# Ninety-six unused bytes: the output stages' left-hand tiles move from 384 to 480 modulo 512

## The chip, the cores and the metric

The kernel runs on one core of one Trainium2 chip. A core has a matrix engine (TensorE, in the profile PE, with its weight loads shown apart as PEld), VectorE (DVE), ScalarE (ACT), GpSimd (POOL) and SyncE (SP), which here issues most of the transfers. [...] The metric is the device time of one execution in microseconds (us).

## The reference, cut to what matters

One layer of a decoder block on 2048 tokens of width 1024. The input is normalised and projected by one wide matrix (`z`); its columns feed a convolution branch and an attention branch. What matters here is the end, where the two branches are projected, gated, added and projected again:

```python
h = rms_norm(x, norm_w) * (1 + scale) + shift
z = h @ w_in                                  # a, b, g_conv, q, k, v, g_attn, m_conv, m_attn
u = silu(layer_norm(causal_conv(a * sigmoid(b)))) * silu(g_conv)
o = attention(q, k, v) * silu(g_attn)         # three dilated windows, merged by their softmax sums
y_conv = u @ w_conv_out                       # 2048 x 1024 by 1024 x 1024
y_attn = o @ w_attn_out                       # 2048 x 512 by 512 x 1024
y = sigmoid(m_conv) * y_conv + sigmoid(m_attn) * y_attn
x = x + gate * (y @ w_out)                    # 2048 x 1024 by 1024 x 1024
```

All inputs and outputs are float32.

## The kernel before, in words

**Precision.** Every large product is made of three passes in a rounded float32 type: each operand is split into a high and a low part (ScalarE copies the high part, VectorE or GpSimd subtracts), and high x high, high x low and low x high are added up in one PSUM bank. So 512 columns of a result over a depth of 128 cost three matmuls of a 128x128 stationary tile against a 128x512 moving tile.

**Stages.** First the projection for q, k, v with attention beside it (matmuls of line 371, moving tiles 384 wide). Then the projections for the gates and for the convolution's input, in blocks by a Strassen-like scheme with seven products (line 897). Then the output stages, with which this case is concerned:

- *Attention projection*, `ya`, line 1203 through the helper `project`: four token blocks `t` of 512 by eight row blocks `dm`; each is 4 x 3 = 12 matmuls, with weights `wah`/`wal` stationary and `ai` moving. The `ai` of block 0 lies in `ai0`, a reused quarter of the hT pools; those of blocks 1 to 3 come from the pools `ua` and `ub` by `parts`.
- *Convolution projection*, `yc`, the same helper: four token blocks by eight row blocks, 8 x 3 = 24 matmuls each, with `wc0` and `wc1` stationary and `u` moving. `u` comes out of the class `Norm` (load, mean, variance, spread, apply), whose steps are hung between the matmuls of the blocks before by `at_block`. `spread` has small matmuls of its own, `pr` (line 1248), that wait for a power computed by GpSimd (`stf`, line 115) from a VectorE copy (line 1241).
- *Output projection*, `oa`, `ob`, `oc`, line 1485: eight quads of seven products with 12 matmuls each; the split `y` is stationary, the weights `wo` are moving. Of the seven weights, B21 and T1 lie in the pool `op`; the others in quarters of the hT pools, in `wcp` and in `lnp`.

**Order.** TensorE's order is the written one (`manual_schedule`). The other engines' queues are ordered by a planner with a simulated timeline, which sees each tile's dependencies; a new tile waits for the old tiles that lay on its bytes (`reuse_waits="tile"`). SyncE issues loads and stores in one queue, so a store that waits for its data holds up the loads behind it.

**Layout.** Pools are stacked from both ends of SBUF. Most open on the left and grow upwards; those with `side="right"` grow downwards from the top. In the layout of the kernel before, the left stack starts at byte 128 with the constants, which have several small tiles and end at 6,016; `sum` takes 8,192 more, up to 14,208, which is 384 modulo 512. When the convolution's pools (`cv`, `gpa`) close at line 1171, the output stages' left-hand pools open from 14,208 on: `gt`, `fr`, `ys`, `ub`, `ua`, and last `ap` (up to 129,120) or, later, `op` in the place of `ua` and `ap`. All tiles below `ap` are multiples of 2,048 bytes, so every matmul operand in `ub`, `ua` and `op` starts at 384 modulo 512. The right stack starts at 229,344, which is 480 modulo 512, and holds tiles of multiples of 512 bytes: all operands of lines 371 and 897, and in the output stages `ai0`, `wah`, `wal`, `wc0`, `wc1` and five of the seven `wo`. Its lowest pool in the output stages is `lnp`, from 131,040.

The matmul of the helper `project`:

```python
        terms = [t for k in range(len(wh)) for t in ((wh[k], xh[k]), (wh[k], xl[k]), (wl[k], xh[k]))]
        for m, (w, xx) in enumerate(terms):
            nc.tensor.matmul(pz, w, xx, start=(m == 0), stop=(m == len(terms) - 1))
```

## Time and profile before

| what | value |
|---|---|
| median of 3 runs | 2399.38 us (2398.85 to 2400.38) |
| profiled execution: time, span | 2401.62 us, 2399.8 us |
| granted TensorE clock, mean | 0.993 |
| TensorE busy | 2356.1 us, 98% |
| VectorE, ScalarE, GpSimd busy | 72%, 43%, 35% |
| first `ya` / first `yc` / first `oa` | 1952 / 2052 / 2240 us |

The profiled execution's span runs from its first to its last instruction. TensorE's matmuls are pipelined: one begins before the one ahead of it has ended, so the duration of a matmul is longer than the spacing from one to the next. The spacing can be read from the chain of work that ended last, where a piece stands for a row of matmuls one behind the other: its length divided by their number. In the groups of instructions, a name such as `ya<-ai_0h,wah` is the result, the moving tile and the stationary tile, with buffer numbers left out.

### The profile page before, as it was taken

To read this page: it belongs to the slowest core of one execution; us is meant where nothing else is said; L and a number is where in the kernel's file an instruction comes from. 1 tells how busy PE (TensorE), PEld (TensorE's weight loads), DVE (VectorE), ACT (ScalarE), POOL (GpSimd) and SP (SyncE) were. 2 spreads that over 40 slices of the span, in tenths; PEclk is the share of its full clock that TensorE was granted. 3 is DMA by queue.
4 is the path that set the end of the run, shared out by engine and by line. 5 is a ranking of instruction groups with operands and counts; after the bars stand their busy time and mean duration, and the time that the engine had idled before them with its cause. 6 is when DMAs were issued, how large, how long until landed. Compare 5 with 4: busy or idle time off the path is not lost.

```text
span 2399.8 us, 38725 instructions
## 1 busy us (share of the span) xinstructions
PE 2356.1 (98%) x12353; PEld 2089.2 (87%) x12353; DVE 1738.8 (72%) x4091; ACT 1022.4 (43%) x2850; POOL 842.7 (35%) x1003
## 2 busy tenths in 40 slices
PE   6999999999999999999999999999999999999999
PEld 2989999999999999998888888788888888878887
DVE  5865655655556777777699999979968778787544
ACT  4733433333444454456444444644444444332221
POOL 3421111111111111123667779656556730000221
PEclk8999999999999999999999999999999999999999
DMA  7633544555552222134545455745444579866552
GB/s 258 216 118 105 163 124 143 155 151 155 165 161 79 65 79 62 55 108 156 169 133 176 154 158 193 239 127 152 141 149 132 167 228 319 288 230 200 177 158 101
DMA packets 354105, 378.56 MB, mean 158 GB/s; under 512 B 29736, under 2 KB 251208, under 8 KB 353902
## 3 DMA queue, kind: packets, MB, share of 16 engines
q1 hardware_dynamic: 316414, 316.64, 42.4%
q10 hardware_dynamic: 37488, 59.46, 7.3%
q8 instruction: 98, 1.61, 0.3%
q14 instruction: 105, 0.86, 0.1%
HBM read 235.34 MB, written 140.64 MB: 157 GB/s over the span
## 4 chain that ended last, share of the span: by engine, by line
PE 87%; DVE 3%; DMA 2%; ACT 2%; issue 1%; POOL 1%; SPq 0%; ACTq 0%; DVEq 0%; POOLq 0%
PE pz L371 29%; PE paab L897 7%; PE yc L1203 6%; PE oa L1485 4%; PE ya L1203 4%; PE pcab L897 4%; PE pag_mc_d L897 4%; PE pag_g_d L897 3%; PE pag_ma_d L897 3%; PE po L500 3%; PE ps L451 3%; PE oc L1485 2%; PE pcg_g_d L897 2%; PE pcg_mc_d L897 2%; PE paag L897 2%; PE pbab L897 2%
## 5 line engine op out<-in xcount | busy, mean ns | idle before, releaser
L371 PE MATMUL pz<-wh_u,hT_lo 128*128 128x384 f32 x1536 | 536.8, 350 | 5.4 <-DVE hT_lo L290 3.6
L371 PE MATMUL pz<-wh_u,hT_hi 128*128 128x384 f32 x1536 | 518.7, 338 | 4.8 <-ACT wh_u L347 2.4
L371 PE MATMUL pz<-wl_u,hT_hi 128*128 128x384 f32 x1536 | 519.2, 338 | 0.4 <-DVE wl_u L350 0.4
L114 POOL TENSOR_SCALAR st<-st 128x2 f32<-128x2 f32 x192 | 48.6, 253 | 809.8 <-ACT sq L388 809.8
L402 DVE SCALAR_TENSOR_TENSOR qk<-pz,st,wqk 128x128 f32<-128x128 f32 x384 | 116.9, 346 | 270.7 <-POOL st L115 269.6
L371 PEld LDWEIGHTS pz<-wh_u,hT_hi 128*128 128x128 f32 x1536 | 291.0, 189 | 8.0 <-ACT wh_u L347 3.3
L371 PEld LDWEIGHTS pz<-wh_u,hT_lo 128*128 128x128 f32 x1536 | 290.0, 189 | 8.3 <-DVE hT_lo L290 4.6
L371 PEld LDWEIGHTS pz<-wl_u,hT_hi 128*128 128x128 f32 x1536 | 290.0, 189 | 1.6 <-DVE wl_u L350 1.1
L443 ACT ACTIVATE qkT<-ptq 128x256 f32<-128x256 f32 x192 | 73.5, 383 | 358.3 <-PE ptq L436 304.0
L975 DVE SCALAR_TENSOR_TENSOR ce<-us,pair_taps,ce 128x512 f32<-128x512 f32 x240 | 180.6, 753 | 6.5
L946 DVE SCALAR_TENSOR_TENSOR ce<-ut,chan,ce 128x512 f32<-128x512 f32 x240 | 178.7, 745 | 0.0
L861 POOL TENSOR_TENSOR slT<-wT,shT 128x512 fp32r<-128x512 f32 x107 | 143.7, 1344 | 81.0 <-ACT shT L860 81.0
L959 DVE SCALAR_TENSOR_TENSOR cq<-ut,chan,cq 128x512 f32<-128x512 f32 x208 | 155.2, 746 | 1.0
L860 ACT ACTIVATE shB<-wB 128x512 fp32r<-128x512 f32 x130 | 82.0, 631 | 162.7 <-PE paab L897 51.7
L115 POOL TENSOR_TENSOR st<-st,mhalf 128x2 f32<-128x2 f32 x192 | 137.3, 715 | 16.0
L388 ACT ACTIVATE sq<-pz 128x128 bf16<-128x128 f32 x384 | 105.6, 275 | 87.5 <-PE pz L371 78.5
L860 ACT ACTIVATE shT<-wT 128x512 fp32r<-128x512 f32 x110 | 69.4, 631 | 163.9 <-POOL wT L852 33.3
L861 POOL TENSOR_TENSOR slB<-wB,shB 128x512 fp32r<-128x512 f32 x85 | 111.0, 1306 | 77.9 <-ACT shB L860 77.4
L500 PE MATMUL po<-lv,pT 128*128 128x128 f32 x596 | 96.8, 274 | 0.0
L500 PEld LDWEIGHTS po<-lv,pT 128*128 128x128 f32 x596 | 90.9, 190 | 0.6 <-issue 0.5
L409 DVE TENSOR_TENSOR t<-qk,tab 128x256 f32<-128x256 f32 x192 | 82.4, 429 | 5.5
L861 POOL TENSOR_TENSOR slT<-wB,shT 128x512 fp32r<-128x512 f32 x57 | 75.1, 1322 | 27.5 <-ACT shT L860 27.4
(742 smaller groups left out, 6162.2 us busy)
## 6 DMA issues: line engine op xcount, KB each, us to landing
wB<-in_w_in_dram SPq DMA_DIRECT2D x154, 256.0 KB, 3.4
qkv_d<-qkv SPq DMA_DIRECT2D x128, 192.0 KB, 2.3
wT<-tT_d SPq DMA_DIRECT2D x88, 256.0 KB, 2.7
raw_u<-in_w_in_dram SPq DMA_DIRECT2D x93, 192.0 KB, 3.4
tT_d<-wB ACTq DMA_DIRECT2D x66, 256.0 KB, 2.3
lqk<-qkv_d SPq DMA_DIRECT2D x128, 128.0 KB, 2.2
acc_d<-osb SPq DMA_DIRECT2D x128, 65.0 KB, 2.0
part<-acc_d ACTq DMA_DIRECT2D x64, 130.0 KB, 2.2
```

Source lines behind the costliest of these rows:

```text
L115: nc.gpsimd.tensor_tensor(dst, scratch[:, :n], mhalf[:, :n], op=ALU.pow)
L371: nc.tensor.matmul(pz[:, :width], part(a, k, P * j, P), w[:, :width], start=(m == 0), stop=(m == 23))
L402: nc.vector.scalar_tensor_tensor(qk[:, 2 * i : 2 * i + 2].rearrange("p a b -> p (a b)"), pz[:, P * i : P * i + P], st[:, 2 + i : 3 + i], w ...
L500: nc.tensor.matmul(po[:, :P], box["pT"][:, P * i : P * i + P], vt, start=(i == 0), stop=(i == nk - 1))
L860: nc.scalar.activation(h, q[name], AF.Copy)
L861: eng.tensor_tensor(l, q[name], h.bitcast(F32), op=ALU.subtract)
L897: nc.tensor.matmul(ps, w, x, start=(m == 0 and ps.name not in first), stop=(m == 11 and not more), skip_group_check=True)
L946: stt(box["e"], e[:, 1 + j : 513 + j], chan[:, cb, 2 * j : 2 * j + 1], box["e"], op0=ALU.mult, op1=ALU.add)
L959: stt(box["o"], o[:, 2 + j : 514 + j], w, psum_o, op0=ALU.mult, op1=ALU.add)
L975: stt(dst, box["both"][:, 1 + j : 513 + j], pair_taps[:, cb, j : j + 1], box["e"], op0=ALU.mult, op1=ALU.subtract if j == 0 else ALU.add)
L1203: nc.tensor.matmul(pz, w, xx, start=(m == 0), stop=(m == len(terms) - 1))
L1485: nc.tensor.matmul(ps, y, w, start=(m == 0 and ps.name not in begun), stop=(m == 11 and not more), skip_group_check=True)
```

## The change

One pool, `level`, is opened on the left just before `gt`, with one tile of 24 float32, that is 96 bytes a partition. Nothing writes or reads it. It stays open to the end of the kernel, so all left-hand pools of the output stages start 96 bytes higher, and their matmul operands lie at 480 modulo 512, as those on the right do. No other line is changed.

```diff
     assert not conv_todo
     gpa_c.__exit__(None, None, None)
     cv_c.__exit__(None, None, None)
+    level = ctx.enter_context(pool("level"))
+    level.tile([P, 24], F32, name="level")
     gp = ctx.enter_context(pool("gt", bufs=3))
     big["fr"] = ctx.enter_context(pool("fr", bufs=2))
     pe_order.__exit__(None, None, None)
```

## The prediction, made before the run

> **What bounds the kernel now.** I read the page first, then the busy time by stretches, the groups of matmuls with shapes kept apart, and last the chain of work that ended last.

> From the page, the span and the busy time of each engine:

> ```profile
> span 2399.8 us, 38725 instructions
> PE 2356.1 (98%) x12353; PEld 2089.2 (87%) x12353; DVE 1738.8 (72%) x4091; ACT 1022.4 (43%) x2850; POOL 842.7 (35%) x1003
> ```

> TensorE is busy for 98% of the span. The shift only concerns the output stages, so what it is worth has to be read there. Busy time of each engine in four stretches of these stages (clock, DMA share and GB/s stand last):

> ```profile
> 1960.00:2100.00 140.00, 140.00 (x622) 113.22 (x621) 106.37 (x173) 55.06 (x90) 4.16 (x6) 1.00 0.91 305
> 2100.00:2146.00 46.00, 44.40 (x193) 35.28 (x193) 38.10 (x59) 14.15 (x23) 1.62 (x2) 1.00 0.68 232
> 2146.00:2240.00 94.00, 94.00 (x407) 75.77 (x407) 68.33 (x104) 28.44 (x49) 5.93 (x4) 1.00 0.59 192
> 2240.00:2396.00 156.00, 156.00 (x671) 125.67 (x669) 78.60 (x114) 30.13 (x53) 37.80 (x28) 1.00 0.46 147
> ```

> From 1960 to 2396 us TensorE idles 1.6 us, all of it in the second stretch, at a granted clock of 1.00; VectorE, the next, is busy 73 to 83% up to 2240 us and 50% after. The last matmul ends at 2396 us and 3.8 us of add and store follow. So a matmul that takes less time moves the end, unless something else becomes late.

> Does the place of the operands cost time? The groups of matmuls from 1930 us on, shapes kept apart; behind the arrow stand moving and stationary tile, and last the busy us, the mean ns of one and the idle time before:

> ```profile
> L1485 PE MATMUL oa<-wohiT,yl 128*128 128x512 f32 x64 | 25.5, 398 | 0.0
> L1485 PE MATMUL oc<-wohiB,yl 128*128 128x512 f32 x32 | 12.8, 399 | 0.0
> L1203 PE MATMUL ya<-ai0hi,wal 128*128 128x512 f32 x32 | 12.5, 390 | 0.0
> L1203 PE MATMUL ya<-ai0lo,wah 128*128 128x512 f32 x32 | 12.5, 389 | 0.0
> L1485 PE MATMUL oc<-wohT,yl 128*128 128x512 f32 x32 | 12.5, 389 | 0.0
> L1485 PE MATMUL ob<-wohB,yl 128*128 128x512 f32 x32 | 12.4, 389 | 0.0
> L1203 PE MATMUL ya<-ai_0h,wal 128*128 128x512 f32 x24 | 9.5, 397 | 0.0
> L1203 PE MATMUL ya<-ai_1l,wah 128*128 128x512 f32 x24 | 9.5, 396 | 0.0
> L1203 PE MATMUL yc<-u_1h,wc1h 128*128 128x512 f32 x16 | 6.4, 397 | 0.0
> ```

> One line, one shape, one stationary tile (wah): with the moving tile ai0, a quarter of the right-hand pools, a matmul has 389 or 390 ns; with ai, a left-hand tile, 396 or 397. In line 1485 the stationary y lies on the left: against a weight on the right (wohiT, wohiB) 398 or 399, against one that also lies on the left (wohT of T1, wohB of B21) 389. Both kinds of equal residue (480 with 480, 384 with 384) are short, and the mixed kind (384 with 480) is long.

> Matmuls overlap, so what counts is the spacing. The chain, start us, us, work; its pieces follow one another without a gap:

> ```profile
> 1800.29 2.72 PE pcab L897 x12
> ...
> 1960.32 7.26 PE ya L1203 x32
> ...
> 2056.27 33.73 PE yc L1203 x144
> ...
> 2146.89 92.78 PE yc L1203 x396
> ...
> 2248.02 2.76 PE ob L1485 x12
> 2250.78 2.81 PE oa L1485 x12
> 2253.60 2.80 PE oc L1485 x12
> ```

> Line 897 (all operands on the right): 2.72/12 = 226.7 ns. ya at 1960 us (ai0 against wah and wal, both on the right): 7.26/32 = 226.9. yc: 33.73/144 = 234.2 and 92.78/396 = 234.3. Out stage, mixed: 2.81/12 = 234.2 and 2.80/12 = 233.3; both on the left: 2.76/12 = 230.0. So a mixed matmul costs 7.5 ns more.

> **The change part by part.** The two new lines issue no instruction on any engine or queue: the tile is never written or read. They add 96 bytes on the left, and everything opened later on the left (gt, fr, ys, ub, ua, ap, later op) starts 96 bytes higher: 384 + 96 = 480. The highest, ap, then ends at 129,216, and the lowest right-hand pool starts at 131,040, so it fits.

> *Attention projection (ya).* Token blocks 1 to 3 have ai on the left: 3 x 8 x 12 = 288 matmuls, at 234.2 - 226.7 = 7.5 ns each 2.16 us. Block 0 (ai0) is on the right already: nothing.

> *Convolution projection (yc).* 4 x 8 x 24 = 768 matmuls, u on the left, wc on the right: 768 x 7.5 ns = 5.76 us.

> *Output projection (oa, ob, oc).* Eight quads of seven products of 12. Five products take a weight from the right: 480 matmuls at (2.805 - 2.72)/12 = 7.1 ns: 3.4 us. B21 and T1 are on the left with y: 192 matmuls at (2.76 - 2.72)/12 = 3.3 ns: 0.64 us. These already have equal residues, yet average 230.0; their lo terms are at 389 ns like the good ones. I take it that they need a few matmuls to fall back into step after a mixed product, and that this ends when no mixed product is left. If not, 0.64 us goes.

> Together 2.16 + 5.76 + 3.4 + 0.64 = 12.0 us of TensorE time.

> *What is late next.* A shorter TensorE stage uncovers whatever is paced otherwise. The only wait of TensorE here, and the chain in front of it:

> ```profile
> PE pr L1248 <- POOL stf L115: 1.6, 1, 1.6
> ```

> ```profile
> 2100.23 0.02 issue
> 2100.25 0.04 DVE mc L1463
> ...
> 2103.81 3.65 DMA gg<-g_d
> ...
> 2135.53 9.13 DMA wo_raw<-in_w_out_dram
> 2144.65 1.03 POOL stf L115
> 2145.73 1.16 PE pr L1248 x8
> ```

> Until 2100 us the chain is TensorE; from there to 2145.7 it runs over VectorE's queue and the loads behind it (gg, then wo_raw), while TensorE has matmuls to do and then stands 1.6 us at pr, waiting for stf, whose copy stood in VectorE's queue. In that stretch TensorE saves 193 x 7.5 ns = 1.45 us, and I take all of that as lost to a longer wait (1.6 + 1.45 = 3.0 us). What is saved before 2100 us reaches this chain through its first link, which is released by yc; what is saved after 2146 us reaches the end. Bounds of this term: nothing lost, even the 1.6 us gone (gain 13.6), or all saved before 2146 us lost: 288 + 372 matmuls x 7.5 ns = 4.95 us (gain 7.0). I take 1.45 because the chain names TensorE up to 2100 us.

> *Order and reuse.* A tile waits for the old tiles under it. In the layout before, the first tiles of gt, fr and ys lie over the same convolution tiles with or without 96 bytes. From ub's fourth slot on (44,928, then 46,976) left-hand tiles straddle two right-hand weight tiles (starting at 45,024 and 47,072); 96 bytes up they meet one. Waits are only taken away, so early loads may move up; I count it as nothing, as TensorE works without a gap over that transition (140.00 of 140 us). The planner may order VectorE and the load queue a little otherwise. The nearest price is the one wait, 1.6 us, either way.

> Sum: 12.0 - 1.45 = 10.5 us. The profiled execution has a span of 2399.8 and a time of 2401.6 us, 2.2 above the median of the runs, 2399.4; from the median, 2388.9; the span should come to about 2389.3.

> [...]

> **The rivals.**

> *A, paced by VectorE and loads until 2146 us.* The 4.95 us saved before that turn into a longer wait at pr. For it: the chain is off TensorE for 45 us, and the DMA share is 0.91 over 140 us. Against: the chain starts at a yc. Gain 7.0: 2392.4.

> *B, half in step.* Equal residues do not settle and everything runs like today's left-left products, 230.0 ns: 1056 x 4.2 ns = 4.4, 480 x 3.75 ns = 1.8, less 193 x 4.2 ns = 0.8 in the wait: 5.4 us, 2394.0. For it: the 2.76 us of ob. Against it: the ya row of 226.9 in the same line.

> *C, no effect.* The 397 come not from the residue but from something that stays, such as the region or the tiles' form: left tiles are 2 KB each, ai0 is part of a larger one. The time stays at 2399.4. Against it: wohT and wohB in the out stage are short next to left-hand y tiles; and the weight tiles of line 897 lie in the very bytes that u and ai take over later.

> *D, slower through transfers.* Transfers to tiles at 480 cost more than at 384 and become the bound of the DMA-heavy stretch. Of the 140 us from 1960 on, 0.91 x 140 = 127 us are DMA busy. 622 matmuls there save some 3.6 of the 12.0 us, so 8.4 are saved after. To end slower by 4.8 us the stretch would have to last 140 + 8.4 + 4.8 = 153 us, so each transfer must grow by 153/127, a fifth; with a quarter it would be 159 us, and the time some 2410. Against it, the DMA issues of the whole run, KB each and median us to landing:

> ```profile
> wT<-tT_d SPq DMA_DIRECT2D x88, 256.0 KB, 2.7
> tT_d<-wB ACTq DMA_DIRECT2D x66, 256.0 KB, 2.3
> out_dram<-xt SPq DMA_DIRECT2D x32, 256.0 KB, 3.0
> ```

> wT and wB are right-hand tiles, at 480, and land no later than xt, a left-hand one at 384.

> **How the numbers follow.** The forecast (2385.8, where the wait goes, to 2390.5, where one more wait of 1.6 us comes) gets 0.58, A 0.20, B 0.10, C 0.08, D 0.04. The predicted time is the forecast's, 2388.9. The range goes from its lower bound to B with half a us for the spread of the runs, 2385.8 to 2394.5, and leaves out C and D, 0.12. About 0.2% (4.8 us) is what a measurement of this kernel tells from no change: faster 0.58 + 0.20 + 0.10 = 0.88, the same 0.08, slower 0.04.

> **What would show it.** Groups of line 1203 with ai and u at 389 or 390 ns, and all of line 1485 there too; chain pieces of 2.72 us for 12 in the out stage; as many matmuls as now, and the rows of lines 371 and 897 unchanged. The wait at pr near 3 us shows the lost term; over 6 us shows A. 393 or so in all groups is B. Unchanged 397 is C. A DMA share near 1 with TensorE idle before 2100 us is D. The prediction is wrong if a new wait of several us opens, or if the projection stages, which share none of the shifted tiles, change their length.

## The result and the profile after

The changed kernel takes 2393.26 us (median of 12 runs, 2388.16 to 2398.87) against 2399.72 us for the kernel before beside it (12 runs, 2397.46 to 2402.32): a ratio of 0.9974, 95% interval 0.9965 to 0.9983, or 6.5 us less by the medians. Its profiled execution has 2392.05 us with a span of 2390.2 us.

The order of instructions on every engine and queue is the same as before; only addresses differ. The groups of matmuls of the changed kernel from 1930 us on (lines 1203 and 1485 of before are 1205 and 1487 here; columns as in the prediction):

```profile
L1487 PE MATMUL oa<-wohiT,yl 128*128 128x512 f32 x64 | 24.9, 389 | 0.0
L1205 PE MATMUL ya<-ai0hi,wal 128*128 128x512 f32 x32 | 12.5, 390 | 0.0
L1487 PE MATMUL oc<-wohT,yl 128*128 128x512 f32 x32 | 12.4, 389 | 0.0
L1487 PE MATMUL ob<-wohB,yl 128*128 128x512 f32 x32 | 12.4, 389 | 0.0
L1487 PE MATMUL oc<-wohiB,yl 128*128 128x512 f32 x32 | 12.4, 389 | 0.0
L1205 PE MATMUL ya<-ai_0h,wal 128*128 128x512 f32 x24 | 9.4, 390 | 0.0
L1205 PE MATMUL yc<-u_1h,wc1h 128*128 128x512 f32 x16 | 6.2, 389 | 0.0
```

All of these rows are at 389 or 390 ns, whichever side their tiles lie on. The chain that ended last shows the spacing:

```profile
2001.33 32.69 PE ya L1205 x144
...
2053.45 24.31 PE yc L1205 x107
...
2082.85 8.17 DMA y_d<-yl
2091.46 5.39 DMA y_d<-yl
2097.32 4.02 DMA y_d<-yl
2101.77 3.50 DMA gg<-g_d
2109.46 8.59 DMA wo_raw<-in_w_out_dram
2132.91 8.90 DMA wo_raw<-in_w_out_dram
2144.04 89.81 PE yc L1205 x396
2233.85 2.72 PE oa L1487 x12
...
2242.01 2.72 PE ob L1487 x12
```

32.69/144 = 227.0 ns, 89.81/396 = 226.8, 2.72/12 = 226.7 in the mixed products and in ob alike. The 396 matmuls of yc that had 92.78 us have 89.81. So the matmuls gave nearly what the prediction summed up, 11.5 of 12.0 us. But the chain now leaves TensorE at 2078 us (24.31 us after 2053.45) instead of 2100, and stays with stores, loads and VectorE until 2143 us. (In the profile of a second execution, `after_again` below, it leaves TensorE at 2096 us, so this point moves from one execution to the next.) TensorE's waits from 1945 us on, in the changed kernel (`pc` are the small matmuls of the variance step, which need `red` from VectorE; `pr` are those of the spread step):

```profile
PE pc L1241 <- DVE red L1235: 2.1, 1, 2.1
PE pr L1250 <- POOL stf L115: 1.3, 1, 1.3
```

Before, there was one, 1.6 us. And the wait at pc has a sequel. Busy time of the engines in three pieces around it (the granted clock is the third number from the end):

```profile
2130.00:2135.00 5.00, 2.89 (x16) 2.19 (x14) 4.39 (x8) 1.26 (x2) 0.00 (x0) 1.00 0.61 192
2135.00:2140.00 5.00, 5.00 (x18) 4.09 (x19) 2.60 (x3) 0.00 (x0) 0.00 (x0) 0.66 1.01 363
2140.00:2145.00 5.00, 4.86 (x26) 3.85 (x25) 4.34 (x7) 0.60 (x1) 1.62 (x2) 1.00 1.03 400
```

After the 2.1 us without work the clock is 0.66 in the mean of the next 5 us (0.50 from 2136 to 2139 us), and only 18 matmuls begin there, some at nearly twice the spacing:

```profile
2136.80 0.63 PE L1205 MATMUL yc<-u_5l,wc1h 128*128 128x512 f32 x1
2137.23 0.63 PE L1205 MATMUL yc<-u_5h,wc1l 128*128 128x512 f32 x1
2137.65 0.63 PE L1205 MATMUL yc<-u_6h,wc1h 128*128 128x512 f32 x1
```

427 ns from one to the next, for eight of them: 8 x 200 ns = 1.6 us more. So TensorE loses 3.7 us there. The end does not come 3.7 us later for it: TensorE reaches the last pr 0.14 us before `stf` is ready, and without the half clock it would, by my estimate from these times, have stood there 1.6 us longer. What sets this release is VectorE's queue. `stf` starts from a VectorE copy of pc, and the copy stands behind the scaling of a load of w_out, for which VectorE stands 3.0 us; pc itself had ended at 2135.55 us:

```profile
2137.40 2.36 DVE L1356 TENSOR_TENSOR wo_raw<-wo_raw,gate 128x1024 f32<-128x1024 f32 x2 [3.01 <-DMA wo_raw<-in_w_out_dram]
2140.88 0.15 DVE L1243 COPY stf<-pc 128x4 f32<-128x4 f32 x1
```

(The chain names a later load, landing at 2141.81 us, as the last link before `stf`. GpSimd's step before it ended at 2141.72 us and the next began 0.08 us later, so it did not stand for that load.)

Counted from the first ya, SyncE issues the load that VectorE stands for after 180.9 us, against 181.0 before, and the last pr begins after 193.0 us, against 193.3. So nearly all that TensorE saves ahead of this pr is lost, whatever form the loss takes on TensorE. From the last pr to the end of the last matmul it is 243.5 us against 250.3: there the saving arrives, 6.8 us. (In the second execution, 191.9 and 243.5 us.)

The account of the profiled executions, from the first ya to the end of the last matmul: 443.6 us before, 436.5 after, 7.1 less. TensorE's spacing gave 11.5 us, the new waits took 3.4 + 0.1 - 1.6 = 1.9, the half clock 1.6 and one slower pair of products from 2250 us on (24 matmuls in 5.69 us in place of 5.44) 0.2; some 0.7 are in small pieces that I did not follow. (The other 2.5 us between the two spans lie before the first ya, in stages that the change does not touch.)

### The profile page after: what moved, and what is told of

The parts are those of the page before. It is cut to its first block, busy times and chain, and to the rows that moved or that the text cites. A ratio compares the mean times of both kernels' runs of the same rounds, so it can differ in the third digit from the quotient of the medians.

```text
span 2390.2 us, 38725 instructions
## 1 busy us (share of the span) xinstructions
PE 2344.7 (98%) x12353; PEld 2087.0 (87%) x12353; DVE 1739.8 (73%) x4091; ACT 1024.5 (43%) x2850; POOL 844.1 (35%) x1003
## 4 chain that ended last, share of the span: by engine, by line
PE 87%; DVE 3%; DMA 3%; ACT 2%; issue 1%; POOL 1%; SPq 0%; ACTq 0%; DVEq 0%; POOLq 0%
PE pz L371 30%; PE paab L897 7%; PE yc L1205 5%; PE pcab L897 4%; PE pag_mc_d L897 4%; PE oa L1487 4%; PE ya L1205 3%; PE pag_g_d L897 3%; PE pag_ma_d L897 3%; PE po L500 3%; PE ps L451 3%; PE pcg_g_d L897 2%; PE oc L1487 2%; PE pbab L897 2%; PE paag L897 2%; PE pcg_mc_d L897 2%
## 5 line engine op out<-in xcount | busy, mean ns | idle before, releaser
L115 POOL TENSOR_TENSOR st<-st,mhalf 128x2 f32<-128x2 f32 x192 | 137.6, 717 | 16.0
## 6 DMA issues: line engine op xcount, KB each, us to landing
wB<-in_w_in_dram SPq DMA_DIRECT2D x154, 256.0 KB, 3.5
wT<-tT_d SPq DMA_DIRECT2D x88, 256.0 KB, 2.7
tT_d<-wB ACTq DMA_DIRECT2D x66, 256.0 KB, 2.3
```

Source lines behind the costliest of these rows:

```text
L115: nc.gpsimd.tensor_tensor(dst, scratch[:, :n], mhalf[:, :n], op=ALU.pow)
```

## The experiments

Theory: what counts is how the two operands lie to each other, and it frees 12 us of TensorE; less arrives because VectorE and the transfers behind it are late from 2078 to 2143 us. Rivals are named with each group. Times are medians; "before" is the kernel before in the same group of runs.

### Which distance?

Four shifts, all with the instructions in the order of the changed kernel:

```diff
-    level.tile([P, 24], F32, name="level")
+    level.tile([P, 40], F32, name="level")     # 160 bytes; 56: 224; 88: 352; 152: 608
```

160 bytes:

> The unused tile has 160 bytes in place of 96, so left-hand operands lie 64 bytes past those on the right (modulo 512). Theory 'whole 512': a matmul is short only where both operands have the same place modulo 512; so ya, yc and the mixed products stay at 230 ns or more from one to the next (12 in 2.76 us or more) and the time is near that of before, 2399. Rival 'shorter period of 64 bytes': all at 226.7 ns (2.72 us for 12), time near 2393. Rival 'any other place than 384 will do': also 226.7.

224 bytes:

> 224 bytes: left-hand operands 128 bytes past those on the right. 'Whole 512': 230 ns or more, time near 2399. Rival 'period 128': 226.7 ns, time near 2393; then 64 bytes must be slow.

352 bytes:

> 352 bytes: left-hand operands 256 bytes past those on the right, half way. 'Whole 512': 230 ns or more, time near 2399. Rival 'period 256': 226.7 ns, time near 2393; then 64 and 128 bytes must be slow.

608 bytes:

> 608 = 96 + 512 bytes: the places modulo 512 are those of the changed kernel, the addresses are not. 'Whole 512': 226.7 ns, 12 matmuls in 2.72 us, time near 2393. Rival 'the period is longer than 512, or it is the address itself': above 226.7 ns.

The same piece of the chain, 144 matmuls of ya, at 160, 224 and 352 bytes, one fence each:

```profile
1999.81 32.96 PE ya L1205 x144
```

```profile
2002.06 33.46 PE ya L1205 x144
```

```profile
2001.83 32.69 PE ya L1205 x144
```

and for 608 bytes, where the chain has no such piece, 396 matmuls of yc:

```profile
2150.86 89.78 PE yc L1205 x396
```

| unused bytes | moving minus stationary in ya and yc | ns from one to the next, ya or yc | mixed product, 12 matmuls | single run, us |
|---|---|---|---|---|
| none (before) | -96 | 234.2 | 2.81 | 2402.89 |
| 96 (changed) | 0 | 227.0 | 2.72 | - |
| 160 | 64 | 228.9 | 2.80 | 2394.55 |
| 224 | 128 | 232.4 | 2.79 | 2396.27 |
| 352 | 256 | 227.0 | 2.72 | 2392.82 |
| 608 | 512 | 226.7 | 2.72 | 2399.39 |

"Whole 512" falls: at 256 bytes, half way, everything is as short as at 0. 64 and 128 bytes are not (228.9 and 232.4 ns), so by these distances the period is 256 bytes. That the side or the address itself counts is excluded too: at 352 and 608 bytes the tiles lie elsewhere, on the left as before, and are short (227.0 and 226.7 ns); and at 160 and 224 bytes, where both operands of ob lie on the left at new places, ob takes 2.74 and 2.73 us for 12 beside mixed products of 2.80 and 2.79. The loss is graded and depends on the direction: with the moving tile 64 bytes past the stationary one 228.9 ns, with it 64 bytes behind (the mixed products at 160 bytes, where y is stationary) 2.80/12 = 233.3. That this is not the stage shows at 224 bytes, where both directions are 128 bytes apart: 232.4 ns in ya and 2.79/12 = 232.5 in the mixed products. The time of the single run at 608 bytes is a miss: I expected 2393. The matmuls are as short as they should be, but this run stood longer at pc, and the 24 matmuls of yc behind it, from 2141.66 us on, had 8.30 us, 346 ns from one to the next:

```profile
PE pc L1241 <- DVE red L1235: 4.3, 1, 4.3
PE oa L1487 <- DVE woloT L1373: 0.5, 1, 0.5
```

That is 2.7 of the 7.4 us by which this span is longer than that of the changed kernel; the other 4.7 lie before the first ya (1954.6 us against 1949.9), in stages that the shift does not touch. From the first ya to the end of the last matmul the profiled executions have 443.6 us before, 436.5 and 435.3 with 96 bytes (two executions), 436.8 with 352, 439.2 with 608, and 440.7 and 440.5 with 160 and 224. So the single times of 160 and 224 bytes, lower than "near 2399", owe a part to an earlier first ya (1948.3 and 1950.2 us against 1952.5 before). The other part is that a slower TensorE waits less (224 bytes: 0.9 us in all; the matmuls of yc with `u_5` to `u_7` stay at 394 to 396 ns there, where some of the changed kernel's have 403 to 405).

### Does putting the waiting steps later help?

```diff
-                    (8, 3, "load"), (9, 3, "mean"), (14, 3, "variance"), (15, 3, "spread")):
+                    (8, 3, "load"), (9, 3, "mean"), (15, 3, "variance"), (16, 3, "spread")):
```

in the changed kernel (late3_after) and in the kernel before (late3_before); with late13_after, in addition:

```diff
-    plan_norm(norms[1], 8, 15, 27, 29, 6)
+    plan_norm(norms[1], 8, 15, 27, 31, 6)
```

The changed kernel again, beside them:

> The changed kernel itself, beside the next two on the same chip. 2393, 6.5 us under the kernel before, with runs further apart than those of before.

Measured: 2393.99 us (before 2400.02), ratio 0.9976 [0.9966, 0.9986]; as expected, though its runs (2391.0 to 2395.4) were not further apart than those of before.

The changed kernel, one block later:

> The changed kernel with the variance and spread steps of the last token block's normalisation hung one row block later (14 and 15 become 15 and 16). Theory 'the loss sits in the two waits': VectorE's queue is late there, TensorE stands 2.1 us at pc and then runs some 3.4 us at half clock; one block later both are gone, and the time is 2389 to 2390. Rival 'the stretch is paced by stores and loads': the waits only move, to pr or to the first matmul that needs the new u, 3 us or more in all, and the time stays at 2393.

Measured: 2394.80 us, 0.9976 [0.9967, 0.9985]. Its waits of TensorE:

```profile
PE pr L1250 <- POOL stf L115: 4.8, 2, 3.9
PE oa L1487 <- DVE woloT L1373: 0.2, 1, 0.2
```

The wait at pc is gone, and 3.9 us stand at the last pr in its place, again with a lower clock behind, 0.66 in the mean from 2145 to 2150 us. The rival was right: the waits move with the steps.

The kernel before, one block later:

> The same step one block later in the kernel before, without the shift. Both theories: its one wait at pr, 1.6 us, goes and nothing else: 2398. Against late3_after it shows what the shift is worth where the waits are out of the way: 'the two waits' 8 to 10 us, 'paced by stores and loads' 5 us.

Measured: 2400.79 us, 0.9997 [0.9989, 1.0006]; no gain, though the wait went down to 0.5 us in the profile. So with these steps late the shift is worth 0.9997 - 0.9976 = 0.0021, 5 us (by the two intervals some 2 to 8), as the rival had it.

Both blocks later:

> As late3_after, and the spread step of the second token block hung two row blocks later too (29 becomes 31), where the changed kernel has its other new wait, 1.3 us at pr. 'The two waits': another 1 us, 2388 to 2389. 'Paced by stores and loads': no gain, since VectorE's work then bunches up later.

Measured: 2397.34 us, 0.9988 [0.9979, 0.9996], worse than the changed kernel beside it by 3.4 us of the medians, though the intervals overlap; 6.2 us stand at the last pr. VectorE's work bunches up, as the rival said.

### What paces the stretch?

In the changed kernel SyncE stands, from 2060 to 2140 us, for 31 us at the load of ya until a store of y from the same slot has landed:

```profile
SPq L1460 <- DMA y_d<-yl: 31.1, 12, 3.9
SPq L1258 <- DVE vf L1264: 7.0, 2, 6.1
```

In the kernel before it stands there too, in the same window:

```profile
SPq L1458 <- DMA y_d<-yl: 27.7, 11, 3.9
```

Two suspects: this slot loop, or the 1 MB loads of w_out that the planner moves up into the stretch, with their scaling on VectorE. The first is changed by a fifth slot:

```diff
-            self.rs = ap.tile([P, 512], F32, tag="rs", name=f"rs{t}")
+            self.rs = ap.tile([P, 512], F32, tag="rs", name=f"rs{t}", bufs=1)
...
-            yt = ys.tile([P, 512], F32, tag="yt", name=f"yt{t}_{dm}", bufs=4)
+            yt = ys.tile([P, 512], F32, tag="yt", name=f"yt{t}_{dm}", bufs=5)   # also for yl and xt
```

> The changed kernel with five instead of four slots for the tiles yt and yl (the room comes from one slot less for rs). Theory 'slot loop': from 2078 us on each load of ya waits for the store of y four blocks earlier to land, SyncE stands 31 us at it, and the gate loads behind it and VectorE are late; with a fifth slot SyncE stands less than 15 us there, TensorE's waits at pc and pr shrink from 3.5 to under 1 us, no stretch at half clock, and the time is 2388 to 2390. Rival 'early weights': the three 1 MB loads of w_out and the scaling of them on VectorE, which the planner puts into this stretch, do it; then the waits and 2393 to 2394 stay.

Measured: 2391.26 us (before 2400.37), 0.9959 [0.9947, 0.9972]. TensorE's waits up to 2145 us, and SyncE's:

```profile
PE pr L1250 <- POOL stf L115: 2.2, 2, 1.5
```

```profile
SPq L1460 <- DMA y_d<-yl: 30.4, 13, 4.1
```

The wait at pc and the half clock are gone (the clock is 1.00 from 2130 to 2145 us), and the time moved the way the slot theory said, short of its 2388 to 2390; with five runs, its interval overlaps that of the changed kernel. The last pr begins 189.7 us after the first ya, 2.2 to 3.3 us sooner than in the two executions of the changed kernel. But SyncE stands as long as before (30.4 us, not under 15), so the reason I gave is not what the run shows. One load of ya now stands earlier in its queue, and the load of w_out that VectorE waits for is issued 178.1 us after the first ya instead of 180.9 (179.9 in the second execution); why it comes sooner I leave open.

The second suspect:

```diff
-        nc.sync.dma_start(w, w_out.rearrange("(h k p) (c n) -> k p h c n", h=2, p=P, c=2)[k])
+        tc.keep_in_program_order(nc.sync.dma_start(w, w_out.rearrange("(h k p) (c n) -> k p h c n", h=2, p=P, c=2)[k]))
```

> The changed kernel with the loads of w_out pinned to their written place in SyncE's queue, two to six row blocks later, so that they and their scaling leave the stretch before the last variance and spread steps. 'Early weights': TensorE's waits at pc and pr shrink from 3.5 to under 1 us and the time is 2388 to 2390. 'Slot loop': the waits and 2393 to 2394 stay.

Measured: 2394.61 us, 0.9978 [0.9969, 0.9987]. The time stays, as "slot loop" said, but not for its reason. TensorE's waits from 1945 us on:

```profile
PE oa L1487 <- DVE xt L1474: 3.8, 1, 3.8
PE oa L1487 <- DVE woloT L1373: 0.5, 1, 0.5
```

None is left at pc or pr, the last pr begins 187.0 us after the first ya instead of 193.0, and the first yc to the first oa take 179.6 us instead of 184.0: in the stretch in question "early weights" holds, for with these loads and their scaling out of VectorE's way the saving arrives (193.3 of before less its wait of 1.6 and the 4.95 us saved is 186.7). What was moved out is late at the next place. The start of the output projection waits 3.8 us for VectorE, then runs at a mean clock of 0.57 for 8 us:

```profile
2238.00:2246.00 8.00, 5.87 (x15) 4.65 (x16) 2.95 (x6) 0.00 (x0) 0.00 (x0) 0.57 0.63 201
```

### The shift with the slot

The fifth slot in the kernel before, and the slot with two of the three loads pinned in the changed one (`keep_in_program_order` only for `k in (1, 2)`):

> The fifth slot for yt and yl without the shift; the instructions stand in the same order as in the changed kernel with five slots (2391.3, 0.9959 of the kernel before). Theory 'the shift buys 12 us of TensorE, and what of it arrives depends on the slack of VectorE and the loads': here TensorE is 12 us slower and has slack enough, so the slot buys only the 1.6 us of the one wait, 2398 to 2400, and with the slot the shift is worth 7 to 10 us instead of 6. Rival 'the slot itself is the gain': 2395 to 2397, and the shift is worth 4 to 6 us with the slot as without.

Measured: 2400.13 us (before 2399.83), ratio 1.0000 [0.9991, 1.0009]. The slot alone buys nothing, so the rival's 2395 to 2397 falls. With the slot the shift is worth 1.0000 - 0.9959 = 0.0041, some 10 us, against 0.0026, 6 us, without. By the intervals that is some 6 to 13 us against 4 to 8, and the two kernels with the slot were measured in different groups of runs: that the slot lets more of the shift arrive is likely, not shown.

> The changed kernel with the fifth slot and with the second and third load of w_out pinned to their written place, so that their scaling leaves VectorE's queue ahead of the last stf. If both fixes add up, the 0.75 us wait at the last pr goes and nothing new comes: 2389 to 2391. If the delayed weights bunch up at the start of the output projection, as with all three pinned (3.8 us of wait at oa and 6.8 us at half clock), 2392 to 2395.

Measured: 2392.02 us, 0.9970 [0.9959, 0.9982]. The wait at the last pr went, as expected, but 0.8 us came at pc, 1.9 us stood at the pr of the second block, which neither fix touches, and 0.8 us came at oa:

```profile
PE pr L1250 <- POOL stf L115: 1.9, 1, 1.9
PE pc L1241 <- DVE red L1235: 0.8, 1, 0.8
PE oa L1489 <- DVE woloT L1375: 0.5, 1, 0.5
PE oa L1489 <- DVE xt L1476: 0.3, 1, 0.3
```

The fixes do not add up. The lowest median of the study is that of the changed kernel with the fifth slot, 2391.26 us; its interval [0.9947, 0.9972] and that of the changed kernel [0.9965, 0.9983] overlap a little.

## Why the prediction was right, and where its size was off

The time lies in the range (2385.8 to 2394.5), and faster is what it forecast; the forecast itself, 2388.9, is 4.4 us too low. The time is above the 2390.5 up to which the forecast's own case went; it is in the range because that was drawn out to B, a case that did not come, so the range held by luck as much as by its reasons.

- *What a matmul saves.* Right in each term: 234.2 to 227.0 ns in ya and yc, 2.81 and 2.80 to 2.72 us in the mixed products. The 0.64 us of the left-left products came too: ob has 2.72 us, so they did need the mixed products gone. Of the 12.0 us summed, the profile shows 11.5.
- *What is late next.* Here is the term that was mis-sized: 1.45 us lost, where about 5 of 11.5 us are lost by the medians. I let the loss begin at 2100 us, because the chain of before named TensorE up to there, and took what is saved earlier to reach the chain through its first link. It did not: the last pr came 193.3 us after the first ya before and 193.0 after (191.9 in the second execution): all but 0.3 to 1.4 us of what TensorE saves ahead of it is lost, from the first ya on, and a second place, pr at 2042 us, waits as well. That is rival A (4.95 us lost, gain 7.0, 2392.4), which had 0.20; the profiles have 7.1 less from the first ya on. By the time alone B's 2394.0 was as near; its 230.0 ns are not there. The sign that I named for A, a wait of over 6 us at the last pr, did not come: the loss sits at pc, at the pr of the block before and in the half clock, and the last pr waits 0.14 us.
- *What a wait costs.* Taken as its own length. The run shows the half clock behind it, 1.6 us on 2.1 us, which at this place only shortens the next wait.
- *Order and reuse.* Right: no instruction changed its place, and nothing opened at the transition into the output stages.
- *Why.* "Equal residues modulo 512" is narrower than what holds: with 256 bytes between the tiles a matmul has 227.0 ns, as with 0.
- *Place alone.* 226.7 to 234.2 ns from one to the next for the same matmul, by the operands' distance alone. What in the chip makes it longer, no run shows.
- *Rivals B, C and D.* Fallen: no group of ya, yc or the output projection at 393 or 397 (those over 400 hold matmuls at half clock or just behind the small ones); the DMA share from 1958 to 2098 us is 0.91 as before, with loads landing in tiles at 480.

## What to carry to other kernels

Read the duration of one form of matmul by where its tiles lie: a difference of 2% within one line and shape, here 397 against 389 ns, was no noise, and an unused tile of 96 bytes removed it. Before counting such a gain as time, look for the last release that a load or another engine paces: what is saved ahead of it can be lost, also ahead of the point where the chain leaves the engine, and here putting the waiting step later only moved the wait. The same saving on its engine was worth 6 us alone and some 10 with a fifth slot, by medians; test a change together with the slack it needs.

## What the runs showed of the hardware that was not expected

Behind some waits of TensorE came a stretch at about half clock: behind 2.1 us at pc 427 ns from one matmul to the next for eight matmuls, with a granted clock of 0.50 from 2136 to 2139 us; behind 3.8 us at oa, with the loads pinned, a mean clock of 0.57 over 8 us; and in the kernel before, behind 2.0 us at `ptq` (line 436) at 1104.8 us, 0.60 up to 1107 us and 0.74 from there to 1110. Other waits of about this length had no such sequel: behind 1.6 us at pr in the kernel before the clock is 1.00 up to 2150 us, and behind 2.0 us at `ptq` in the changed kernel, at 1101.9 us, it is 1.00 from 1102 to 1108. So the length of the wait alone does not decide it, and what does is not shown here.
